# Hybrid encoder trunk: the mixers' input renewed ahead of the values, and half of the mixing weights' second parts made by a copy and an adding transfer

## The chip, the cores and the metric

One core of a Trainium2 chip. The metric is device time in microseconds (us) of one execution; a kernel's time is the median of three runs, and beside them stands one profiled execution, from which every row of the trace is taken.

## The reference

Two layers over an input of 512 tokens and 1024 channels. In each, three token mixers read the same normed input, their outputs are merged by gates, and a feed-forward block and an embedding gate follow.

```python
h = rmsnorm(x, mix_norm[i])
z = h @ w_in[i]
u_rnn, u_gelu, c_q, ckv_rope, fq, fk, fv, f_logit, gate_logit = split_columns(z)
y_a = rglru_branch(u_rnn, u_gelu, ...) @ w_br_a[i]     # causal conv of width 4, gates, recurrence
y_b = mla_branch(c_q, ckv_rope, ...) @ w_br_b[i]       # latent attention, 8 heads
y_c = fox_branch(fq, fk, fv, f_logit, fox_bf[i]) @ w_br_c[i]  # 8 heads, forget-gate bias
g = sigmoid(gate_logit + gate_b[i]).reshape(B, S, 3, D)
merged = g[:, :, 0] * y_a + g[:, :, 1] * y_b + g[:, :, 2] * y_c
x = x + merged @ w_o[i]
...                                                     # SwiGLU block, then x += sigmoid(.) * (p[i] @ w_ple[i])
```

The recurrence is `h = a h + b` with `a = exp(log_a)` and `b = sqrt(1 - a^2) * (gate * conv)`. All is float32.

## The kernel before, in words

**Precision.** A float32 operand is held as two float32r parts, first (`h`, hi) and second (`l`, lo = value minus first). Each product of a 128x128 weight tile with 128x512 of activations is three matmuls (`mm3`): hi by hi, hi by lo, lo by hi.

**Weights.** All weights come as one stream of 606 units, each of four tiles (128x512, 256 KB). SP's queue loads a unit into `raw` (4 slots). `Stream._split` makes the parts in `hl` (8 slots): ScalarE casts the first (line 112), VectorE subtracts for the second (line 113). `_ensure` splits unit u+7 when unit u is begun.

**Pages.** Activations lie in SBUF pages: `pf` (20 of 128x512 float32) and `pr` (31 of two float32r parts). Eight PSUM banks of 128x512.

**One layer's mixing** (`mix`). The input of the mixers is eight pages X, made at first without the norm's factor: x times the gain, split. The factor per token, r (a page `st["r"]`, as a column `rT`), is known only later, so that what is computed from X is multiplied by r when it leaves PSUM ("rescaled"). In program order: four tile columns for the convolution branch (u), the packed columns of rotary key and forget logits, four for the gelu branch (ug), the recurrence's gates, `lru_tail` (square roots, products and scans of the recurrence, with the last of VectorE's scans at line 677), key and query of the first head pair (`fox_proj`), the values of the fox attention (`values`: eight units of 12 matmuls, into four banks at once), then `attention`. `lru_tail` stands ahead of the first heads in the kernel before already.

**Attention** runs over head and query block; each step does the scores, the softmax (VectorE, ScalarE) and, with TensorE free meanwhile, some tiles of independent work taken from a plan: `fp(p, w)` is key or query of head pair p, `mg(n, j)` a merge gate with its branch column, `lq` and `lkv` latent projections.

**Renewal.** `renorm(ks)` loads x again from DRAM through POOL's queue, multiplies it by gain and r (line 218, a scalar_tensor_tensor on VectorE) and splits it (line 233 on ScalarE, line 221 on VectorE) into new pages Xn. Nothing computed from Xn needs rescaling. In the kernel before it stands in three pieces in the first plan of the fox attention, between fills that still use X and r; `drop_x` then frees X and r.

**Order.** Each engine works through its instructions in order. A framework's scheduler sets that order per engine from the program and its dependences; `high_priority` around the weight splits lets them go ahead. Where below the order of an engine is printed, a row is line, operation, output and inputs, and what it waits for (an engine's count, with the suffix of its semaphore); `DMASW` is a transfer issued by POOL, `DMAHW` one issued by SP. `bank_67` to `bank_74` are the PSUM banks.

Of the kernel before, what the change touches and what calls it, by code (L numbers as in the profile page):

```python
# [10 lines left out]
F32 = mybir.dt.float32  # L11
F32R = mybir.dt.float32r
I32 = mybir.dt.int32
AF = mybir.ActivationFunctionType
ALU = mybir.AluOpType
# [3 lines left out]
KD = D // 128  # L19
# [18 lines left out]

NUNITS = 606
KEPT = NUNITS - 16  # L40
PACKED = (8, 9, 311, 312)


# [41 lines left out]
class Stream:  # L85
# [15 lines left out]
    def _split(self, u):  # L101
        s = (u % self.nraw) * 512
        src = self.raw[:, s:s + 512]
        if u >= KEPT:
            self.kept[u] = self.pages.take()
        hi, lo = self._parts(u)
        if u in PACKED:
            hi, lo = (x.rearrange("p (k c) -> p k c", c=128)[:, :, 64 * i:64 * i + 64]
                      for i, x in ((0, hi), (1, hi)))
            src = src.rearrange("p (k c) -> p k c", c=128)[:, :, 0:64]  # L110
        with self.tc.high_priority():
            self.nc.scalar.copy(hi, src)  # L112
            self.nc.vector.tensor_tensor(lo, src, hi.bitcast(F32), op=ALU.subtract)  # L113

    def _parts(self, u, c=slice(0, 512)):
        if u in self.kept:
# [5 lines left out]
    def _ensure(self, u):  # L122
        last = min(u + self.nhl - 1, max(u + 4, KEPT - 1), NUNITS - 1)
        while self.loaded < min(self.nraw, NUNITS):
            self._load(self.loaded)
            self.loaded += 1
        while self.done <= last:
            self._split(self.done)
            self.done += 1
            while self.loaded < min(self.done + self.nraw, NUNITS):  # L130
                self._load(self.loaded)
                self.loaded += 1
# [34 lines left out]
class Trunk:  # L167
# [273 lines left out]
    def mix(self, layer):  # L441
        nc = self.nc
        L, st, X = layer, self.st, self.xp
# [42 lines left out]
        rT = self.cols(NT)  # L486
# [24 lines left out]
        def key_and_forget():  # L511
# [3 lines left out]
            for k, x in enumerate(X):  # L515
                assert self.w.pos // 4 in PACKED
                wh, _ = self.w.tile(("kf", L, k))
# [84 lines left out]
        def fox_proj(p, X, r):  # L602
            return [
                self.dense(self.win(L, C_FK + 128 * p), X, ev_heads(kp, p, r, True, False)),
                self.dense(self.win(L, C_FQ + 128 * p), X, ev_heads(qp, p, r, True, True)),
            ]

        def values(spec, X, rT):

            V = []  # L610
            bs = [self.banks.take() for _ in range(NT)]
            for k, x in enumerate(X):
                wh, wl = self.w.wide(spec + (k,))
                for j in range(NT):
                    c = slice(j * 128, (j + 1) * 128)
                    self.mm3(bs[j][:, :], x.h[:, c], x.l[:, c], wh, wl, k == 0, k == len(X) - 1)
                    yield
            for j in range(NT):
                g = pr.take()
                V.append(g)  # L620
                dst = g.ap.rearrange("p (h t d) -> p h t d", h=HEADS, t=2)
                src = bs[j].rearrange("p (h d) -> p h d", h=HEADS)
                hi = dst[:, :, 0, :]
                if rT is None:
                    self.split(hi, dst[:, :, 1, :], src)
                else:
                    r = rT[:, j:j + 1]
                    self.act(hi, src, AF.Copy, scale=r)
                    self.stt(dst[:, :, 1, :], src, r, hi.bitcast(F32), ALU.mult, ALU.subtract)
                self.banks.give(bs[j])  # L630
            self.V = V


        yA = [None] * 4
# [50 lines left out]
        k0, q0 = fox_proj(0, X, st["r"])  # L685
        self.run(k0)
        self.run(q0)
        self.run(values(("fv", L), X, rT))
        Xn = [None] * KD

        def renorm(*ks):

            for k in ks:
                t, p = pf.take(), pr.take()
                nc.gpsimd.dma_start(t.ap, x_dram[k])
                self.stt(t.ap, t.ap, self.v(L, V_MIX + k), st["r"].ap, ALU.mult, ALU.mult)
                self.split(p.h, p.l, t.ap)
                t.free()
                Xn[k] = p
            return  # L700
            yield

        def drop_x():
            for p in X:
                p.free()
            st.pop("r").free()
            return
            yield


        merged = [None] * KD
        out_pages = [None] * KD
# [32 lines left out]
        def merge(n, j, ys, X=Xn, r=None):  # L745
            box = []
            yield from gate(n, j, box, X, r)
            yield from branch(n, j, ys, box)
# [154 lines left out]
        def fp(p, w, X=Xn, r=None):  # L903
            return (fox_proj(p, X, r)[w], 8)

        def mg(n, j, ys, X=Xn, r=None):
            return (merge(n, j, ys, X, r), 12)
# [56 lines left out]
        def done_c():  # L964
            for p in oC:
# [5 lines left out]
        lkv = [(latent(ckv, skv, C_CKV, j), 8) for j in range(2)]  # L971
        tail = chain(gate(2, 2, boxes[2, 2]), gate(2, 3, boxes[2, 3]))
        attention(True, oC, [
            [fp(1, 0, X, st["r"]), (renorm(0, 1), 0), mg(0, 0, yA, X, st["r"]), (renorm(2, 3, 4), 0),
             mg(0, 1, yA, X, st["r"]), (renorm(5, 6, 7), 0), (drop_x(), 0), fp(1, 1), mg(0, 2, yA)],
            [fp(2, 0), mg(0, 3, yA), mg(0, 4, yA), fp(2, 1), mg(0, 5, yA)],
            [fp(3, 0), mg(0, 6, yA), fp(3, 1)] + lq,
            lkv + [mg(0, 7, yA), (free_yA(), 0), (latent_sums(), 0), gt(2, 0), (latent_norm(), 0),
# [160 lines left out]
    def ple_last(self, X, pw):  # L1139

        L, st = DEPTH - 1, self.st
        self.w.align()
        assert self.w.pos == 4 * KEPT
        fin = [{}, {}]
        half = [slice(0, SEQ // 2), slice(SEQ // 2, SEQ)]

        def part(i, j):
            t = half[i]
            b = self.banks.take()
            for k in range(KD):  # L1150
                if i == 0:
                    wh, wl = self.w.tile(("w_ple_gate", L, 128 * j, 128, k))
                else:
                    wh, wl = self.w.again(4 * KEPT + KD * j + k)
                self.mm3(b[:, :SEQ // 2], wh, wl, X[k].h[:, t], X[k].l[:, t], k == 0, k == KD - 1)
# [236 lines left out]
```

## Time and profile before

| | |
|---|---|
| median of three runs | 1826.25 us (1825.64 to 1828.06) |
| the profiled execution | 1826.21 us; span 1824.4 us, granted clock 0.994 |
| matmul records | 8476 |
| stream of weights (SP's queue) | 606 loads of 256 KB |
| second parts by subtraction (line 113) | 590 records, 404.4 us of VectorE |
| first parts by cast (line 112) | 590 records, 363.8 us of ScalarE |

A page row of busy time gives for each engine us, share of the span and number of instructions. Timeline rows give start, length, engine, line, operation, output and inputs, how many, and in brackets the idle time ahead with what ended it. PE is TensorE's matmul, PEld its weight load, DVE VectorE, ACT ScalarE, POOL GpSimd. Granted clock is the share of TensorE's full clock.

### The profile page before, as it was taken

Reading aid. Unit: us, or ns where it says so; the run is one execution under the profiler, and the core shown is the slowest. Engines: PE = TensorE matmul, PEld = TensorE weight load, DVE = VectorE, ACT = ScalarE, POOL = GpSimd, SP = SyncE. Lnnn points to the kernel's source line nnn. Section 1 sums busy time; section 2 is a strip of 40 time slices with the busy share of each in tenths; the row PEclk is TensorE's granted clock in tenths of the full one; section 3 lists DMA queues with packets and bytes.
Section 4 is the critical chain, followed back from the end, with each engine's and each line's share of the span. In section 5 each row is a group of like instructions: output and inputs, shape, how many; then the busy total and the mean of one; then the engine's idle time right before and its main releaser. Section 6 shows DMA issues by size and latency. Waiting matters only on the chain. (4 is left out here: it accounts for less than half of the span.)

```text
span 1824.4 us, 24163 instructions
## 1 busy us (share of the span) xinstructions
PE 1803.9 (99%) x8476; PEld 1504.5 (82%) x8476; DVE 1209.1 (66%) x2421; ACT 817.5 (45%) x1562; POOL 116.8 (6%) x234
## 2 busy tenths in 40 slices
PE   9899999999999999999999999999999999999998
PEld 7688888888888888888888788888888888888887
DVE  8896678866665555444778966888576555553457
ACT  5766556553333333223448655565523333332233
POOL 1230001100000000000103200010000000000000
PEclk9899999999999999999999999999999999999999
DMA  6142224324322233322433322342232323232331
GB/s 206 59 150 83 81 78 116 100 70 139 95 96 95 96 99 98 109 95 98 133 111 123 105 81 82 90 117 85 87 128 92 99 98 97 95 110 99 98 99 47
DMA packets 98826, 184.17 MB, mean 101 GB/s; under 512 B 13552, under 2 KB 14752, under 8 KB 98704
## 3 DMA queue, kind: packets, MB, share of 16 engines
q1 hardware_dynamic: 89280, 162.04, 27.3%
q0 software_dynamic: 8416, 19.45, 3.9%
q8 instruction: 66, 1.08, 0.2%
q10 hardware_dynamic: 1008, 1.14, 0.2%
q14 instruction: 56, 0.46, 0.1%
HBM read 173.98 MB, written 4.21 MB: 98 GB/s over the span
## 5 line engine op out<-in xcount | busy, mean ns | idle before, releaser
L237 PE MATMUL bank<-pr,hl 128*128 128x512 f32 (+1 forms) x6812 | 1602.3, 392 | 7.0 <-ACT pr L233 6.9
L237 PEld LDWEIGHTS bank<-pr,hl 128*128 128x128 f32 (+1 forms) x6812 | 1270.0, 188 | 268.9 <-ACT pr L233 8.6
L112 ACT CAST hl<-raw 128x512 fp32r<-128x512 f32 x590 | 363.8, 618 | 649.4 <-PE bank L237 438.8
L113 DVE TENSOR_TENSOR hl<-raw,hl 128x512 fp32r<-128x512 f32 x590 | 404.4, 686 | 367.9 <-ACT hl L112 352.0
L221 DVE TENSOR_TENSOR pf<-pf 128x512 f32<-128x512 f32 (+3 forms) x235 | 151.2, 651 | 31.9 <-ACT pf L230 29.8
L221 DVE TENSOR_TENSOR pf<-bank,pf 128x512 f32<-128x512 f32 (+3 forms) x198 | 132.9, 676 | 56.9 <-PE bank L237 31.9
L230 ACT ACTIVATE pf<-pf 128x512 f32<-128x512 f32 (+1 forms) x145 | 86.0, 600 | 112.3 <-DVE pf L221 110.0
L237 PE MATMUL bank<-pr 128*128 128x256 f32 (+5 forms) x704 | 119.5, 301 | 3.5 <-ACT pf L230 3.3
L237 PEld LDWEIGHTS bank<-pr 128*128 128x128 f32 (+1 forms) x704 | 103.4, 190 | 13.7 <-ACT pf L230 3.4
L221 DVE TENSOR_TENSOR pr<-pf,pr 128x512 fp32r<-128x512 f32 (+3 forms) x126 | 85.5, 683 | 4.0 <-ACT pr L233 3.1
L230 ACT ACTIVATE pf<-bank,small 128x384 f32<-128x384 f32 (+3 forms) x130 | 68.9, 531 | 42.0 <-DVE small L838 38.6
L233 ACT CAST pr<-pf 128x512 fp32r<-128x512 f32 (+2 forms) x114 | 70.3, 620 | 29.2 <-DVE pf L218 18.1
L855 ACT CAST pth<-bank 128x128 fp32r<-128x128 f32 (+3 forms) x128 | 54.0, 426 | 65.4 <-PE bank L830 62.3
L838 DVE TENSOR_REDUCE small<-bank 128x1 f32<-128x384 f32 (+3 forms) x128 | 61.7, 484 | 19.2 <-PE bank L237 18.2
L221 DVE TENSOR_TENSOR ptl<-bank,pth 128x128 fp32r<-128x128 f32 (+3 forms) x128 | 61.7, 484 | 12.8 <-ACT pth L855 10.3
L237 PE MATMUL bank<-hl,pr 128*128 128x512 f32 x240 | 55.9, 390 | 0.0
L830 PE MATMUL bank<-identr,pf 128*128 128x128 f32 x320 | 55.7, 273 | 0.0
L237 PEld LDWEIGHTS bank<-hl,pr 128*128 128x128 f32 x240 | 44.9, 188 | 9.2
L225 DVE TENSOR_SCALAR pf<-pf,small 128x384 f32<-128x384 f32 (+3 forms) x128 | 48.4, 383 | 2.6
L230 ACT ACTIVATE pf<-bank,vec 128x512 f32<-128x512 f32 x60 | 41.0, 688 | 16.7 <-PE bank L237 16.2
L218 DVE SCALAR_TENSOR_TENSOR pf<-pf,bank 128x512 f32<-128x512 f32 x48 | 32.6, 683 | 20.8 <-PE bank L237 20.5
L830 PEld LDWEIGHTS bank<-identr,pf 128*128 128x128 f32 x320 | 40.0, 141 | 7.6
(112 smaller groups left out, 792.9 us busy)
## 6 DMA issues: line engine op xcount, KB each, us to landing
raw<-wst SPq DMA_DIRECT2D x606, 256.0 KB, 2.6
pf<-xT POOLq DMA_DIRECT2D x16, 256.0 KB, 3.1
pr<-pr POOLq DMA_DIRECT2D x32, 128.0 KB, 2.7
pf<-xs POOLq DMA_DIRECT2D x16, 256.0 KB, 3.1
pf<-trig POOLq DMA_DIRECT2D x12, 256.0 KB, 3.1
pf<-xT SPq DMA_DIRECT2D x8, 256.0 KB, 5.4
xs<-pf POOLq DMA_DIRECT2D x8, 256.0 KB, 2.7
pf<-pT POOLq DMA_DIRECT2D x4, 256.0 KB, 3.1
```

The source lines that it names most:

```text
L112: self.nc.scalar.copy(hi, src)
L113: self.nc.vector.tensor_tensor(lo, src, hi.bitcast(F32), op=ALU.subtract)
L218: self.nc.vector.scalar_tensor_tensor(out, a, s, b, op0=op0, op1=op1)
L221: self.nc.vector.tensor_tensor(out, a, b, op=op)
L225: self.nc.vector.tensor_scalar(out, a, s1, None, op0=op0)
L230: return self.nc.scalar.activation(out, a, f, **kw)
L233: self.nc.scalar.copy(hi, src)
L237: self.nc.tensor.matmul(out, a, b, start=start, stop=stop, skip_group_check=True)
L830: nc.tensor.transpose(T[:, c], p2.ap[:, c], self.ident[:, :])
L838: nc.vector.reduce_max(R[t][:, 0:1], S[:, :m], axis=AX.X, negate=True)
L855: self.nc.scalar.copy(hi, src)
```

## The change

Two edits. First, units in `ADDED` (every odd unit from 11 to 129 and from 315 to 433, 120 of 606, those of the two layers' mixing) get their second part in another way: ScalarE writes minus the first part into the second's place, and a transfer issued by POOL adds the unit's weights from DRAM to it. VectorE's subtraction is left out for these; the cast and the load into `raw` stay. Second, the renewal of all eight pages stands ahead of the values, X and r are dropped behind them, and the fills of the first plan that used X and r (one projection and two merges per layer) read Xn and lose their rescaling.

```diff
--- before.py
+++ after.py
@@ -38,6 +38,8 @@
 
 NUNITS = 606
 KEPT = NUNITS - 16
+
+ADDED = {*range(11, 130, 2), *range(315, 434, 2)}
 PACKED = (8, 9, 311, 312)
 
 
@@ -110,7 +112,13 @@
             src = src.rearrange("p (k c) -> p k c", c=128)[:, :, 0:64]
         with self.tc.high_priority():
             self.nc.scalar.copy(hi, src)
-            self.nc.vector.tensor_tensor(lo, src, hi.bitcast(F32), op=ALU.subtract)
+            if u in ADDED:
+
+                self.nc.scalar.activation(lo, hi.bitcast(F32), AF.Copy, scale=-1.0)
+                c = 512 * (u % 2)
+                self.nc.gpsimd.dma_start(lo, self.wdram[u // 2][:, c:c + 512], accum_op=ALU.add)
+            else:
+                self.nc.vector.tensor_tensor(lo, src, hi.bitcast(F32), op=ALU.subtract)
 
     def _parts(self, u, c=slice(0, 512)):
         if u in self.kept:
@@ -685,7 +693,6 @@
         k0, q0 = fox_proj(0, X, st["r"])
         self.run(k0)
         self.run(q0)
-        self.run(values(("fv", L), X, rT))
         Xn = [None] * KD
 
         def renorm(*ks):
@@ -697,16 +704,15 @@
                 self.split(p.h, p.l, t.ap)
                 t.free()
                 Xn[k] = p
-            return
-            yield
 
         def drop_x():
             for p in X:
                 p.free()
             st.pop("r").free()
-            return
-            yield
-
+
+        renorm(*range(KD))
+        self.run(values(("fv", L), X, rT))
+        drop_x()
 
         merged = [None] * KD
         out_pages = [None] * KD
@@ -971,8 +977,7 @@
         lkv = [(latent(ckv, skv, C_CKV, j), 8) for j in range(2)]
         tail = chain(gate(2, 2, boxes[2, 2]), gate(2, 3, boxes[2, 3]))
         attention(True, oC, [
-            [fp(1, 0, X, st["r"]), (renorm(0, 1), 0), mg(0, 0, yA, X, st["r"]), (renorm(2, 3, 4), 0),
-             mg(0, 1, yA, X, st["r"]), (renorm(5, 6, 7), 0), (drop_x(), 0), fp(1, 1), mg(0, 2, yA)],
+            [fp(1, 0), mg(0, 0, yA), mg(0, 1, yA), fp(1, 1), mg(0, 2, yA)],
             [fp(2, 0), mg(0, 3, yA), mg(0, 4, yA), fp(2, 1), mg(0, 5, yA)],
             [fp(3, 0), mg(0, 6, yA), fp(3, 1)] + lq,
             lkv + [mg(0, 7, yA), (free_yA(), 0), (latent_sums(), 0), gt(2, 0), (latent_norm(), 0),
```

The lines move by 8 behind the first edit: 113 becomes 121, 218 becomes 226, 221 becomes 229, 233 becomes 241, 237 becomes 245, 677 becomes 685, 695 becomes 702.

What moves on the engines, at three places in layer 0. TensorE, from the last block of the values on; `bank<-hl,pr` rows are values, `bank<-pr` rows are attention scores, and `bank<-pr,hl` rows are fills. Before:

```order
L237 MATMUL bank_72<-hl,pr 128x512 x3
L237 MATMUL bank_73<-pr 128x128 [waits Activation_49]
L237 MATMUL bank_73<-pr 128x128 [waits DMASW0_49,DMASW2_49,DVE_49,Pool_49]
L237 MATMUL bank_68<-pr,hl 128x512 x21
L237 MATMUL bank_69<-pr 128x256 x2
L237 MATMUL bank_68<-pr,hl 128x512 x3
L237 MATMUL bank_70<-pr,hl 128x512 x14
L237 MATMUL bank_70<-pr,hl 128x512 [waits DVE_49]
L237 MATMUL bank_70<-pr,hl 128x512 x3
L237 MATMUL bank_71<-pr 128x384 [waits DVE_49]
```

and now:

```order
L245 MATMUL bank_72<-hl,pr 128x512 x3
L245 MATMUL bank_73<-pr 128x128 [waits DVE_49,Activation_49]
L245 MATMUL bank_68<-pr,hl 128x512
L245 MATMUL bank_68<-pr,hl 128x512 [waits DVE_49]
L245 MATMUL bank_68<-pr,hl 128x512
L245 MATMUL bank_69<-pr 128x256
L245 MATMUL bank_70<-pr,hl 128x512 [waits DVE_49]
L245 MATMUL bank_70<-pr,hl 128x512
L245 MATMUL bank_70<-pr,hl 128x512 [waits DVE_49]
L245 MATMUL bank_73<-pr 128x128 [waits DMASW1_49,DMASW3_49,DVE_49,Pool_49]
L245 MATMUL bank_69<-pr 128x256
L245 MATMUL bank_71<-pr 128x384 [waits DVE_49]
```

Before, the first fill (bank_68) goes through all its blocks of X without a wait, 24 matmuls, and the second follows it; now the first blocks of two fills (banks 68 and 70) are followed by work that waits for VectorE. Further on, the second parts of the first fill's second block (the last row) stand behind more waits for VectorE, and wait for it themselves:

```order
L245 MATMUL bank_72<-pr,hl 128x512 [waits DVE_49]
L245 MATMUL bank_72<-pr,hl 128x512
L245 MATMUL bank_72<-pr,hl 128x512 [waits DMASW5_49]
L245 MATMUL bank_67<-pr,hl 128x512 [waits DVE_49]
L245 MATMUL bank_67<-pr,hl 128x512
L245 MATMUL bank_68<-pr,hl 128x512 [waits Activation_49]
L245 MATMUL bank_70<-pr,hl 128x512
L245 MATMUL bank_72<-pr,hl 128x512
L245 MATMUL bank_73<-pr 128x512 [waits Activation_49]
L245 MATMUL bank_73<-pr 128x512
L245 MATMUL bank_68<-pr,hl 128x512 [waits DVE_49]
```

VectorE, where the values leave their banks (`pr<-bank,small,pr` rows). `pf<-pf,vec` rows are the multiplication of a renewed page, `pr<-pf,pr` rows the second half of a split, and `hl<-raw,hl` rows the weight subtraction. Before:

```order
L218 SCALAR_TENSOR_TENSOR pf<-pf,vec 128x512 [waits DMASW1_49]
L113 TENSOR_TENSOR hl<-raw,hl 128x512 [waits DMAHW7_49,Activation_49]
L218 SCALAR_TENSOR_TENSOR pf<-pf,vec 128x512 [waits DMASW2_49]
L218 SCALAR_TENSOR_TENSOR pr<-bank_71,small,pr 128x8x64 [waits Activation_49]
L221 TENSOR_TENSOR pr<-pf,pr 128x512 [waits Activation_49]
L218 SCALAR_TENSOR_TENSOR pr<-bank_74,small,pr 128x8x64 [waits Activation_49]
L221 TENSOR_TENSOR bank_73<-bank_73,fmask 128x128 [waits PE_49]
L218 SCALAR_TENSOR_TENSOR pf<-pf,vec 128x512 [waits DMASW3_49]
L218 SCALAR_TENSOR_TENSOR pr<-bank_67,small,pr 128x8x64 [waits Activation_49]
L221 TENSOR_TENSOR pr<-pf,pr 128x512 [waits Activation_49]
L113 TENSOR_TENSOR hl<-raw,hl 128x512 [waits DMAHW0_49,Activation_49]
```

and now:

```order
L226 SCALAR_TENSOR_TENSOR pr<-bank_74,small,pr 128x8x64 [waits Activation_49]
L226 SCALAR_TENSOR_TENSOR pr<-bank_67,small,pr 128x8x64 [waits Activation_49]
L226 SCALAR_TENSOR_TENSOR pr<-bank_72,small,pr 128x8x64 [waits PE_49,Activation_49]
L229 TENSOR_TENSOR bank_73<-bank_73,fmask 128x128 [waits PE_49]
L229 TENSOR_TENSOR bank_69<-bank_69,fmask 128x128 [waits PE_49]
L226 SCALAR_TENSOR_TENSOR pf<-pf,vec 128x512 [waits DMASW3_49]
L229 TENSOR_TENSOR pr<-pf,pr 128x512 [waits Activation_49]
L229 TENSOR_TENSOR bank_71<-bank_71,fmask 128x128 [waits DVE_49,PE_49]
L226 SCALAR_TENSOR_TENSOR pf<-pf,vec 128x512 [waits DMASW4_49]
L844 TENSOR_REDUCE small<-bank_73 128x1 [waits DVE_49]
L844 TENSOR_REDUCE small<-bank_69 128x1 [waits DVE_49]
L229 TENSOR_TENSOR pr<-pf,pr 128x512 [waits Activation_49]
```

Ahead of the first row shown stands the evacuation of the first bank. Of the renewal's eight multiplications six stand ahead of it now and two behind it, five and three before; the last row is the split of page 1, the second of the eight. From the first `SCALAR_TENSOR_TENSOR` of the recurrence behind the scan of the forget gates (line 537, now 545) to this row stand 55 instructions, both counted: 4 scans, 8 multiplications of renewed pages, 4 evacuations of values, 3 masks, 2 reductions, 5 weight subtractions and 29 others of 512 columns.

POOL, around the forget gates' logarithm (lines 376 to 379, now 384 to 387). Before:

```order
L378 TENSOR_SCALAR pf<-pf 128x32 [waits Pool_49]
L379 TENSOR_TENSOR pf<-pf 128x32 [waits Pool_49]
L534 DMA pf<-pf 8x16x32 [waits DVE_49,Activation_49]
L589 DMA pr<-pr 2x1x512 [waits DMASW0_49,DVE_49]
L589 DMA pr<-pr 2x1x512 [waits DMASW1_49]
```

and now:

```order
L386 TENSOR_SCALAR pf<-pf 128x32 [waits Pool_49]
L387 TENSOR_TENSOR pf<-pf 128x32 [waits Pool_49]
L542 DMA pf<-pf 8x16x32 [waits DMASW7_49,DVE_49]
L119 DMA hl<-wst 128x512 [waits DMASW0_49,PE_49,Activation_49]
L702 DMA pf<-xT 128x512 [waits DMASW7_49,DMASW1_49]
L595 MEMSET pr 4x512 [waits PE_49,Pool_49]
L119 DMA hl<-wst 128x512 [waits DMASW2_49,Activation_49]
L702 DMA pf<-xT 128x512 [waits DMASW3_49,DVE_49]
L702 DMA pf<-xT 128x512 [waits DMASW4_49]
```

The eight loads of x (line 695) stood in one run behind six small transfers of the head pages (line 589), two of which are shown. Now they (line 702) follow the logarithm's transfer at once, with adding transfers (line 119) and memsets of the head pages between them; the first add shown is that of unit 27, which waited its turn behind the whole logarithm.

## The prediction

> **What bounds the kernel now.** I read the engine shares first, then TensorE's waits, then windows and timelines around the places that these point to.
>
> The page, busy time and slices:
>
> ```profile
> PE 1803.9 (99%) x8476; PEld 1504.5 (82%) x8476; DVE 1209.1 (66%) x2421; ACT 817.5 (45%) x1562; POOL 116.8 (6%) x234
> ...
> PEclk9899999999999999999999999999999999999999
> ```
>
> The waits of TensorE (us in total, times, longest):
>
> ```profile
> PE bank L237 <- ACT pr L233: 6.9, 3, 3.8
> PE bank L237 <- ACT pf L230: 3.3, 1, 3.3
> PE bank L237 <- DVE one L385: 1.0, 1, 1.0
> PE bank L237 <- ACT raw L230: 0.9, 1, 0.9
> ```
>
> TensorE is the bound. The first two rows are all that matters inside the program; the third belongs to its start, the fourth to its end. A change that touches no matmul can win only there, so its value must be read from two places. The windows of 8 us at them (columns: PE, PEld, DVE, ACT, POOL, granted clock, DMA share, GB/s), with one undisturbed window first:
>
> ```profile
> 44.00:52.00 8.00, 8.00 (x37) 6.63 (x36) 8.00 (x16) 4.54 (x8) 0.63 (x1) 1.00 0.15 44
> 52.00:60.00 8.00, 3.65 (x15) 2.36 (x13) 8.00 (x15) 3.78 (x7) 0.00 (x0) 0.98 0.24 71
> 60.00:68.00 8.00, 5.47 (x12) 3.87 (x13) 8.00 (x15) 4.89 (x8) 0.00 (x0) 0.50 0.18 61
> 68.00:76.00 8.00, 8.00 (x32) 6.48 (x32) 5.18 (x11) 8.00 (x15) 4.90 (x13) 0.88 0.13 35
> ...
> 1018.00:1026.00 8.00, 4.83 (x14) 3.85 (x15) 7.91 (x16) 5.13 (x11) 3.29 (x7) 0.79 0.34 107
> ```
>
> 37 matmuls go into 8 us, 0.216 us each. Layer 0 lost 111-59 = 52 of them from 52 to 76, 11.2 us: 6.9 of waiting and 4.3 of clock at 0.50. Layer 1 lost 23, 5.0 us: 3.3 of waiting, 1.7 of clock. So the prize is 16.2 us at most. VectorE is full (8.00 of 8) in both. TensorE's timeline:
>
> ```profile
> 49.77 5.15 PE L237 MATMUL bank<-pr,hl 128*128 128x512 f32 x22
> 58.72 0.73 PE L237 MATMUL bank<-pr,hl 128*128 128x512 f32 x2 [3.81 <-ACT pr L233]
> 60.69 1.22 PE L237 MATMUL bank<-pr,hl 128*128 128x512 f32 x2 [1.23 <-ACT pr L233]
> 63.75 18.61 PE L237 MATMUL bank<-pr,hl 128*128 128x512 f32 x68 [1.84 <-ACT pr L233]
> 82.21 21.92 PE L237 MATMUL bank<-hl,pr 128*128 128x512 f32 x96
> 103.97 0.33 PE L237 MATMUL bank<-pr 128*128 128x128 f32 x2
> ...
> 975.84 21.92 PE L237 MATMUL bank<-hl,pr 128*128 128x512 f32 x96
> 997.60 0.22 PE L237 MATMUL bank<-pr 128*128 128x128 f32 x1
> ...
> 1021.17 0.73 PE L237 MATMUL bank<-pr 128*128 128x512 f32 x2 [3.29 <-ACT pf L230]
> ```
>
> The x96 blocks are the values. Behind them TensorE finds attention work ready at once, since its first fills read the old X pages. VectorE at the same time (the POOL rows are the logarithm that precedes the scan of the forget gates):
>
> ```profile
> 70.08 0.31 POOL L376 TENSOR_SCALAR pf<-pf 128x32 f32<-128x32 f32 x1 [23.90 <-DVE pf L221]
> 77.67 0.25 POOL L379 TENSOR_TENSOR pf<-pf 128x32 f32<-128x32 f32 x1
> 79.03 0.71 POOL L534 DMA_DIRECT2D pf<-pf  x1 [1.10 <-DVE pf L218]
> ...
> 81.14 1.22 DVE L537 TENSOR_TENSOR_SCAN pf<-one,pf 8x512 f32<-8x512 f32 x1 [0.78 <-DMA pf<-pf]
> 82.39 0.69 DVE L113 TENSOR_TENSOR hl<-raw,hl 128x512 fp32r<-128x512 f32 x1
> 85.31 1.31 DVE L218 SCALAR_TENSOR_TENSOR pf<-pf 128x512 f32<-128x512 f32 x2 [0.79 <-ACT pf L230]
> 92.10 1.22 DVE L677 TENSOR_TENSOR_SCAN pf<-pf 128x512 f32<-128x512 f32 x1
> 93.24 0.66 DVE L113 TENSOR_TENSOR hl<-raw,hl 128x512 fp32r<-128x512 f32 x1
> 93.82 0.68 DVE L218 SCALAR_TENSOR_TENSOR pf<-bank,pf 128x512 f32<-128x512 f32 x1
> 94.42 0.68 DVE L113 TENSOR_TENSOR hl<-raw,hl 128x512 fp32r<-128x512 f32 x1
> ...
> 111.75 0.28 DVE L221 TENSOR_TENSOR bank<-bank,fmask 128x128 f32<-128x128 f32 x1
> 111.95 0.73 DVE L218 SCALAR_TENSOR_TENSOR pf<-pf,vec 128x512 f32<-128x512 f32 x1
> 112.61 0.74 DVE L218 SCALAR_TENSOR_TENSOR pr<-bank,small,pr 128x512 fp32r<-128x512 f32 x1
> ...
> 982.38 1.29 DVE L218 SCALAR_TENSOR_TENSOR pf<-pf 128x512 f32<-128x512 f32 x2
> ```
>
> The 85.31 row begins the recurrence (the products behind the square roots); call its start T. In layer 1 T is 982.38. From start to start, a scan takes 1.14 us, a plain 128x512 operation 0.60, one with a per-partition column (`vec`, `small`) 0.66, a mask 0.20.
>
> **The adding transfers.** 120 subtractions leave VectorE, 120 negated copies join ScalarE, 120 transfers join POOL's queue. Prices:
>
> ```profile
> L113 DVE TENSOR_TENSOR hl<-raw,hl 128x512 fp32r<-128x512 f32 x590 | 404.4, 686 | 367.9 <-ACT hl L112 352.0
> L230 ACT ACTIVATE pf<-pf 128x512 f32<-128x512 f32 (+1 forms) x145 | 86.0, 600 | 112.3 <-DVE pf L221 110.0
> ...
> pf<-xT POOLq DMA_DIRECT2D x16, 256.0 KB, 3.1
> ...
> pf<-xT SPq DMA_DIRECT2D x8, 256.0 KB, 5.4
> ```
>
> VectorE loses 120 x 0.686 = 82 us, ScalarE gains 120 x 0.600 = 72, POOL at most 120 x 0.71 = 85 of issuing (the 79.03 row). All of it lies beside TensorE except where the two stalls are: cost 0. No row shows an adding transfer. The nearest are 3.1 us (256 KB on POOL) and 5.4 (256 KB on SP at the start); I take 3.1, the same queue. The cover is the lead: a unit is split 7 units ahead of its 12 matmuls, 7 x 12 x 0.216 = 18 us. Behind a busy POOL the add can come late. The tightest is unit 27, queued behind the logarithm (some 8 us), with a landing at about 82, while TensorE wants its second part in the fourth value block, 80.4 + 3 x 2.74 = 88.6. That leaves 6 us; at 5.4 us a landing 4 are left. Gone, it would be a wait of TensorE for each microsecond over, in every unit of that stretch.
>
> A page of the Trainium skill speaks against such transfers: SBUF — State Buffer, "SBUF: two separate sides", says that a transfer issued from GpSimd needs descriptors written through a port that VectorE's two-port operations lock, and gives about 3.1 us in place of 0.62 for one that overlaps such an operation. By it an add here might land some 2.5 us later (estimate), and the sum would not move, but the chance of rival (c) would be some 0.2. The x pages land in 3.1 us although VectorE is full while they come, so the trace does not bear the rule out, and (c) keeps 0.10.
>
> **The convolution's end, layer 0.** TensorE waits at 54.9 to 63.75 for splits behind a full VectorE. In the new order two subtractions fewer (2 x 0.60) stand ahead of them, and the first result reaches VectorE three matmuls earlier (3 x 0.216): 1.8 us, between 0 and 3. The values then end at 103.97 - 1.8 = 102.2.
>
> **The renewal, layer 0.** The new first fills read the renewed pages. The first fill may use page 0 early, but its second block wants page 1, whose split is the last but one of the renewal on VectorE, behind the four evacuations of the values. From T to that split VectorE has 55 instructions: 4 scans, 12 of 0.66, 5 masks and reductions of about 0.22, 34 of 0.60 (5 of them weight subtractions): 4.6 + 7.9 + 1.1 + 20.4 = 34.0. T itself is not set by VectorE's load but by the logarithm, its transfer and the scan: 1.8 us earlier, two memsets inside POOL's chain (0.3 each, its other rows' size), and no subtraction between scan and T: 70.08-1.8+7.84+0.6 = 76.7, transfer issued at 77.9, landed 2.1 later as before (79.03 to 81.14), scan 1.2: T = 81.4 (80 to 84; the late end if ScalarE, 8.00 of 8 from 68 to 76, with its negated copies holds the square roots back). Page 1 is ready at 115.4. TensorE without a wait would stand there 32 matmuls behind the values, six of them narrow: 102.2 + 6.3 = 108.5. New wait: 6.9, in pieces of which the longest is some 4.
>
> **The renewal, layer 1.** Values end at 997.60 as before, since TensorE did not wait ahead of them. VectorE's share from T to page 1's split is 60 instructions, 13 short ones: 4 x 1.14 + 12 x 0.66 + 31 x 0.60 + 13 x 0.25 = 34.3. T is bounded by ScalarE and the scan; fewer subtractions let the logarithm start sooner, ScalarE's square roots hardly: 980.4 (979 to 982.4). Ready at 1014.7; TensorE would be there at 997.6 + 35 matmuls, 7.0, = 1004.6. New wait 10.1. The old loss of 5.0 goes: the heads' VectorE work then no longer competes with the renewal.
>
> **Clock.** Idle time lowers the clock: 4.3 us lost in layer 0 beside 6.9 of waiting, 1.7 in layer 1 beside 3.3. For the new waits I take 2.0 and 2.5, nearest to the second since most of the slow stretch falls into the waiting; bounds 0 and 4.3 each.
>
> The Trainium skill, TensorE: Matmul & The Clock Gate, "What's actually happening", has the half clock after an idle window of about 3.4 us and until a busy one of 3.4. By that each place would lose about 1.7 us (estimate), and the sum would come out 1.1 us lower. The trace agrees in layer 1 (1.7) but not in layer 0 (4.3), where short bursts lay between waits.
>
> **The rescaled evacuations.** Three groups per layer lose an operation of 0.60 on VectorE, inside the count above. POOL loads the eight x pages in both; they land before their turn.
>
> **Sum.** Layer 0: -1.8 + 6.9 + 2.0 = +7.1. Layer 1: -5.0 + 10.1 + 2.5 = +7.6. The profiled execution took 1826.2 us (span 1824.4 and 1.8 around it), equal to the median of 1826.25. 1826.2 + 14.7 = 1840.9, say 1841. Its own range, with all low ends and all high ends: -3.0+5.5-5.0+8.7 = +6 and 9.5+4.3-5.0+12.1+4.3 = +25: 1832 to 1851.
>
> **Rivals.** (a) Faster: the relief of VectorE pulls T forward so far that all pages are renewed under the values. It decides if T is at 74.5 and 970.3 or sooner with the same 34 us. Then the two stalls shrink by 1.8 and 5.0 and nothing new comes: 1819.4. For it: 82 us off VectorE where it is full. Against it: VectorE is already idle 0.78 and 0.79 ahead of scan and T, waiting for a transfer and ScalarE.
> (b) No change: the new waits come out near 3.4 us each with little clock, since TensorE's first fills find some pages early; gains and waits cancel at 1826. That needs T 4 to 6 us sooner than I have it.
> (c) Much slower: the adding transfers land late, behind POOL's in-order waits or because an add is dearer than a copy. The point is 6 us more at unit 27, or over 5.2 us each if they go one after another (a unit pair lasts 24 x 0.216). One microsecond over that in all 120 is +120; only behind the logarithm, two units per layer, about +10: 1851, and I call 1860 its time. Only the 5.4 row speaks for it.
> (d) The adds come to nothing, VectorE being no faster at the places that count: that is my own forecast but for the 1.8; 1843, inside its range.
>
> **Chances.** Forecast with (d) 0.69, (a) 0.13, (b) 0.08, (c) 0.10. A measurement tells 0.2%, 3.7 us, from no change. Faster 0.13, same 0.08, slower 0.79. The range 1825 to 1855 holds forecast, (b) and the mild part of (c); outside are (a) and the dear part of (c).
>
> **What would show it.** Right: a TensorE wait for L229 or L241 pieces of 4 us and more behind each values block, at about 104 and 1000; VectorE at 8.00 of 8 from T to 115; the 1021 wait gone; adds landing in about 3 us and no wait for a transfer. Wrong: no wait behind the values (T early), or waits for `hl` from a transfer.

## The result and the profile after

The changed kernel takes 1842.59 us (median of 4 runs, 1840.59 to 1843.63) where the kernel before takes 1827.13 on the same count (1825.64 to 1828.06): a ratio of 1.0084, 95% interval 1.0067 to 1.0102. It is slower by 15.5 us. The profiled execution took 1840.59 us, its span is 1838.8, 14.4 more than before.

The page of the changed kernel, busy time and the adding transfers (KB each, median us from issue to landing):

```profile
PE 1809.2 (98%) x8476; PEld 1506.4 (82%) x8476; DVE 1140.6 (62%) x2295; ACT 881.0 (48%) x1682; POOL 219.5 (12%) x354
...
hl<-wst POOLq DMA_DIRECT2D x120, 256.0 KB, 4.2
```

VectorE lost 68.5 us of work (1209.1 to 1140.6), and the kernel is slower all the same. TensorE's waits (us in total, times, longest) say where:

```profile
PE bank L245 <- DVE pr L226: 12.6, 4, 6.9
PE bank L245 <- ACT pr L241: 5.7, 5, 2.3
...
PE bank L245 <- DVE pr L229: 0.8, 1, 0.8
```

The first and the last row are new. There line 226 on VectorE is the evacuation of the values out of their banks, and line 229 the split of a renewed page. The waits at the convolution's end (line 241 in layer 0) are smaller, and the 3.3 us wait of layer 1 for the softmax is gone. The windows (PE, PEld, DVE, ACT, POOL, clock, DMA share, GB/s):

```profile
52.00:60.00 8.00, 4.57 (x17) 2.92 (x16) 8.00 (x15) 4.74 (x9) 0.85 (x1) 0.94 0.66 149
60.00:68.00 8.00, 7.36 (x21) 5.04 (x21) 7.55 (x17) 6.59 (x11) 0.41 (x2) 0.63 0.04 15
...
100.00:108.00 8.00, 2.76 (x13) 1.87 (x12) 7.94 (x13) 7.09 (x14) 4.31 (x10) 0.93 0.97 237
108.00:116.00 8.00, 5.44 (x12) 3.97 (x13) 8.00 (x17) 2.49 (x4) 1.83 (x4) 0.50 0.43 110
...
1006.00:1014.00 8.00, 2.66 (x10) 1.61 (x9) 8.00 (x15) 6.23 (x12) 3.14 (x6) 0.84 1.08 308
1014.00:1022.00 8.00, 6.37 (x19) 4.54 (x17) 8.00 (x19) 5.41 (x12) 1.48 (x3) 0.74 0.15 41
```

From 52 to 68 there are 38 matmuls in place of 27. From 100 to 116 there are 25, where 37 go into each 8 us undisturbed. VectorE is full or nearly so in all of them (7.55 of 8 at the least). TensorE's timeline, both layers:

```profile
61.42 17.50 PE L245 MATMUL bank<-pr,hl 128*128 128x512 f32 x66 [0.64 <-ACT pr L241]
78.76 21.92 PE L245 MATMUL bank<-hl,pr 128*128 128x512 f32 x96
...
102.85 0.47 PE L245 MATMUL bank<-pr 68*128 68x128 f32 x2 [0.56 <-issue]
110.25 1.01 PE L245 MATMUL bank<-pr 128*128 128x384 f32 x2 [6.94 <-DVE pr L226]
111.57 6.96 PE L245 MATMUL bank<-pr,hl 128*128 128x512 f32 x18 [0.31 <-DVE pr L226]
...
118.83 5.38 PE L245 MATMUL bank<-pr,hl 128*128 128x512 f32 x23
...
983.23 21.92 PE L245 MATMUL bank<-hl,pr 128*128 128x512 f32 x96
1010.66 0.62 PE L245 MATMUL bank<-pr 128*128 128x384 f32 x2 [3.88 <-DVE pr L226]
...
1012.97 5.44 PE L245 MATMUL bank<-pr,hl 128*128 128x512 f32 x12 [1.46 <-DVE pr L226]
...
1021.19 0.98 PE L245 MATMUL bank<-pr,hl 128*128 128x512 f32 x3 [1.63 <-ACT pr L241]
...
1023.78 10.49 PE L245 MATMUL bank<-pr,hl 128*128 128x512 f32 x45 [0.76 <-DVE pr L229]
```

The values start 3.45 us earlier in layer 0 (82.21 to 78.76) and 7.39 later in layer 1 (975.84 to 983.23), so layer 0 cost 7.4 us net; the other 7.0 of the 14.4 come in layer 1. VectorE at the start of the recurrence, at the evacuation of the values and at the split of page 1:

```profile
79.53 1.22 DVE L545 TENSOR_TENSOR_SCAN pf<-one,pf 8x512 f32<-8x512 f32 x1 [2.01 <-DMA pf<-pf]
80.78 1.29 DVE L226 SCALAR_TENSOR_TENSOR pf<-pf 128x512 f32<-128x512 f32 x2
...
109.45 2.72 DVE L226 SCALAR_TENSOR_TENSOR pr<-bank,small,pr 128x512 fp32r<-128x512 f32 x4
...
115.14 0.69 DVE L229 TENSOR_TENSOR pr<-pf,pr 128x512 fp32r<-128x512 f32 x1
...
984.55 1.22 DVE L545 TENSOR_TENSOR_SCAN pf<-one,pf 8x512 f32<-8x512 f32 x1 [2.84 <-DMA pf<-pf]
...
988.49 0.75 DVE L226 SCALAR_TENSOR_TENSOR pf<-pf,vec 128x512 f32<-128x512 f32 x1 [1.29 <-DMA pf<-xs]
989.16 1.29 DVE L226 SCALAR_TENSOR_TENSOR pf<-pf 128x512 f32<-128x512 f32 x2
...
1023.03 1.30 DVE L229 TENSOR_TENSOR pr<-pf,pr 128x512 fp32r<-128x512 f32 x2
```

From the first product of the recurrence to the end of page 1's split VectorE works 35.0 us in layer 0 (80.78 to 115.8) and 34.5 in layer 1 (989.16 to 1023.7) without a pause. TensorE has stood still or gone slowly since 103 and 1007.

### The profile page after: what moved, and what is told of

Same layout as the page of the kernel before. It is cut to its first block, busy times and chain, and to the rows that moved or that the text cites. A ratio compares the mean times of both kernels' runs of the same rounds, so it can differ in the third digit from the quotient of the medians.

```text
span 1838.8 us, 24284 instructions
## 1 busy us (share of the span) xinstructions
PE 1809.2 (98%) x8476; PEld 1506.4 (82%) x8476; DVE 1140.6 (62%) x2295; ACT 881.0 (48%) x1682; POOL 219.5 (12%) x354
## 4 chain that ended last, share of the span: by engine, by line
PE 93%; DVE 4%; POOL 1%; DMA 1%; issue 1%; ACT 0%; DVEq 0%; POOLq 0%
PE bank L245 91%; PE bank L836 2%; DVE pf L226 1%; DVE pr L229 1%; DVE pf L685 0%; DVE pf L229 0%; DMA pf<-pf 0%; DVE hl L121 0%; POOL pf L386 0%; POOL pf L387 0%; DVE pr L226 0%; DMA pf<-xs 0%; ACT pr L574 0%; ACT hl L114 0%; DVE small L844 0%
## 5 line engine op out<-in xcount | busy, mean ns | idle before, releaser
L121 DVE TENSOR_TENSOR hl<-raw,hl 128x512 fp32r<-128x512 f32 (+1 forms) x470 | 322.8, 687 | 358.1 <-ACT hl L114 342.6
L229 DVE TENSOR_TENSOR pf<-pf 128x512 f32<-128x512 f32 (+3 forms) x235 | 151.7, 653 | 31.7 <-ACT pf L238 29.5
L229 DVE TENSOR_TENSOR pf<-bank,pf 128x512 f32<-128x512 f32 (+3 forms) x192 | 128.9, 677 | 63.6 <-PE bank L245 31.6
L119 POOL DMA_DIRECT2D hl<-wst x120 | 107.0, 892 | 478.8 <-ACT hl L117 380.7
L245 PE MATMUL bank<-pr 128*128 128x256 f32 (+4 forms) x704 | 120.6, 302 | 11.4 <-DVE pr L226 10.8
L229 DVE TENSOR_TENSOR pr<-pf,pr 128x512 fp32r<-128x512 f32 (+2 forms) x122 | 82.6, 684 | 6.9 <-ACT pr L241 6.3
L238 ACT ACTIVATE pf<-bank,small 128x512 f32<-128x512 f32 (+3 forms) x130 | 69.0, 532 | 32.8 <-DVE small L844 29.0
L241 ACT CAST pr<-pf 128x512 fp32r<-128x512 f32 (+1 forms) x114 | 70.0, 618 | 28.8 <-DVE pf L226 17.8
L229 DVE TENSOR_TENSOR ptl<-bank,pth 128x128 fp32r<-128x128 f32 (+3 forms) x128 | 61.9, 487 | 25.2 <-ACT pth L861 20.9
L844 DVE TENSOR_REDUCE small<-bank 128x1 f32<-128x128 f32 (+3 forms) x128 | 62.2, 488 | 24.4 <-PE bank L245 23.1
L117 ACT ACTIVATE hl<-hl 128x512 fp32r<-128x512 f32 x120 | 75.9, 632 | 2.0
L229 DVE TENSOR_TENSOR bank<-bank,fmask 128x128 f32<-128x128 f32 x64 | 19.0, 298 | 54.5 <-PE bank L245 54.0
```

What stands on the lines that cost most here:

```text
L117: self.nc.scalar.activation(lo, hi.bitcast(F32), AF.Copy, scale=-1.0)
L119: self.nc.gpsimd.dma_start(lo, self.wdram[u // 2][:, c:c + 512], accum_op=ALU.add)
L229: self.nc.vector.tensor_tensor(out, a, b, op=op)
L238: return self.nc.scalar.activation(out, a, f, **kw)
L245: self.nc.tensor.matmul(out, a, b, start=start, stop=stop, skip_group_check=True)
L844: nc.vector.reduce_max(R[t][:, 0:1], S[:, :m], axis=AX.X, negate=True)
```

## Experiments

Theory A: the adding transfers cost nothing and win a few us at both old stalls; the loss is the renewal, because the first fills now read pages that VectorE finishes late. Its rivals are that the adds make the loss (B), that VectorE is late for the values' evacuation whatever TensorE reads (C), and that POOL's queue delivers late once more is asked of it (D). The adds alone, the renewal alone, the early renewal with fills on X, and the adds in two places are set against 16 runs of the kernel before (1826.14 us median), the other four against 12 runs (1826.34).

### The adds alone

```diff
# the kernel before, with
+ADDED = {*range(11, 130, 2), *range(315, 434, 2)}
 ...
+            if u in ADDED:
+                self.nc.scalar.activation(lo, hi.bitcast(F32), AF.Copy, scale=-1.0)
+                c = 512 * (u % 2)
+                self.nc.gpsimd.dma_start(lo, self.wdram[u // 2][:, c:c + 512], accum_op=ALU.add)
+            else:
                 # the subtraction on VectorE, as before
```

> The adding transfers alone; the renewal and the first plan stand as in the kernel before. Theory A (the loss comes from the renewed pages, the adds cost nothing): the values of layer 0 start at 78.8 as in the changed kernel (82.2 before), no wait for VectorE behind the values, the wait at 1021 smaller or gone: 1827 - 3.4 - (0 to 5) = 1819 to 1824. Rival B (the adds themselves cost TensorE, by late landings or a busy ScalarE): 1827 or more, with waits for a transfer or for ScalarE's cast that the kernel before does not have.

Measured: 1818.92 us, ratio 0.9959 (0.9947 to 0.9972). TensorE's waits inside the program are one row, and the values stand at

```profile
PE bank L245 <- ACT pr L241: 2.9, 2, 2.3
```

```profile
80.42 21.92 PE L245 MATMUL bank<-hl,pr 128*128 128x512 f32 x96
...
973.40 21.92 PE L245 MATMUL bank<-hl,pr 128*128 128x512 f32 x96
```

The values start 1.8 us earlier in layer 0, as the prediction had it (the expectation had 3.4, from the changed kernel's own trace, and the time is at the low end of its range). The wait at 1021 is gone and no other takes its place. Theory A holds for this half: the adds are worth 7 us. B falls.

### The renewal alone

```diff
# the changed kernel, with
-ADDED = {*range(11, 130, 2), *range(315, 434, 2)}
+ADDED = set()
```

> The renewal ahead of the values alone; all second parts are subtracted on VectorE as before. Theory A: the recurrence starts at 85.3 as before, and VectorE has 4 subtractions more (2.4 us) in front of page 1: ready at 85.3 + 34.2 + 2.4 = 121.9 where TensorE would stand at 110.3, so 11.6 of waiting and 2 to 4 of clock in layer 0; in layer 1 982.4 + 36.7 = 1019 against 1004.6, 14.5 and 2 to 4, less the old 5.0: 1827 + 25 to 29 = 1852 to 1856. Rival B (the adds make the loss): about 1827.

Measured: 1847.88 us, ratio 1.0118 (1.0104 to 1.0132), 22 us slower. The waits and the values:

```profile
PE bank L245 <- DVE pr L226: 10.7, 4, 5.7
PE bank L245 <- ACT pr L241: 8.2, 4, 3.8
PE bank L245 <- POOL pr L595: 4.2, 1, 4.2
```

```profile
80.91 21.92 PE L245 MATMUL bank<-hl,pr 128*128 128x512 f32 x96
...
120.95 5.28 PE L245 MATMUL bank<-pr,hl 128*128 128x512 f32 x22 [0.64 <-DVE pr L229]
...
985.43 21.92 PE L245 MATMUL bank<-hl,pr 128*128 128x512 f32 x96
```

The sign and the place are those of theory A, the size is 4 us below the expected range. The miss lies in layer 0, which costs 9.6 net (975.84 to 985.43) where 13.6 to 15.6 was expected; layer 1 costs the other 12.2, inside its 11.5 to 13.5. In layer 0 the reader of page 1 goes on at 120.95, 12.0 us after the 109.0 (80.91 + 21.76 + 6.3) at which TensorE could have been there, and its last wait is for page 1's split. So the lateness is about the expected 11.6, the slow clock lies inside it, and I had added 2 to 4 for the clock on top. Ahead of the values 1.3 us were won (last section), and 1.1 come back behind, by what is open. The third row, a wait for POOL to clear a head page in layer 1, is not what sets the loss: a wait for a split (L229) ends behind it, at 1029.6. The two halves nearly add up: -7.2 for the adds and +21.7 for the renewal make 14.5, against 15.5 for both.

### The renewal early, but the first fills read X

```diff
# the changed kernel, with (drop_x is a step of the plan again)
-        drop_x()
 ...
-            [fp(1, 0), mg(0, 0, yA), mg(0, 1, yA), fp(1, 1), mg(0, 2, yA)],
+            [fp(1, 0, X, st["r"]), mg(0, 0, yA, X, st["r"]), mg(0, 1, yA, X, st["r"]), (drop_x(), 0), fp(1, 1), mg(0, 2, yA)],
```

> The changed kernel with adds and with all eight pages renewed ahead of the values, but the first projection and the first two merges read X and are rescaled by r as before, and X is dropped behind them. VectorE's order up to the evacuation of the values is that of the changed kernel. Theory A (TensorE waits since its first fills read renewed pages and since only three short fills stand ahead of the score that needs the first bank of the values): the 7 us waits behind both values go, the gain of 3.4 at the convolution's end stays, the old wait at 1021 may come back: 1819 to 1824. Rival C (the renewal ahead of the values keeps VectorE so long that the evacuation of the values itself is late, whatever TensorE reads): TensorE still waits 5 us and more for the first bank in each layer, 1830 to 1840.

Measured: 1820.73 us, ratio 0.9969 (0.9957 to 0.9982). The waits, and VectorE's evacuation of the first banks in layer 0:

```profile
PE bank L245 <- ACT pr L241: 4.4, 4, 2.3
PE bank L245 <- ACT pf L238: 1.1, 1, 1.1
```

```profile
110.35 2.06 DVE L226 SCALAR_TENSOR_TENSOR pr<-bank,small,pr 128x512 fp32r<-128x512 f32 x3
```

VectorE still evacuates the values late (110.35 in layer 0, 109.45 in the changed kernel), and no wait for it is left: the score that waited 6.94 us for the first bank now stands behind 46 matmuls, nearly all of them fills on X, in place of 10. So an early renewal does next to no harm by itself (1820.73 against 1818.92 with the adds alone), C falls, and what costs is that the first fills need its result. This one edit takes back 22 us.

### One fill in three reads X

```diff
# the changed kernel, with (drop_x is a step of the plan again)
-        drop_x()
 ...
-            [fp(1, 0), mg(0, 0, yA), mg(0, 1, yA), fp(1, 1), mg(0, 2, yA)],
+            [fp(1, 0, X, st["r"]), (drop_x(), 0), mg(0, 0, yA), mg(0, 1, yA), fp(1, 1), mg(0, 2, yA)],
```

> The changed kernel, but the first projection of the first plan (24 matmuls, 5.2 us) reads X and is rescaled; the two merges behind it read the renewed pages. Theory A (the loss is the time by which VectorE's renewal ends later than TensorE runs out of other work, so each fill that does not need it takes its own length off): some 21 matmuls or 4.5 us more lie ahead of the first renewed block in each layer, so the loss falls by 4.5 and a part of the clock's per layer: 1842.5 - 9 to 13 = 1829 to 1833. Rival C (any fill that reads renewed pages stops TensorE as long as before): 1838 to 1843.

Measured: 1832.43 us, ratio 1.0032 (1.0020 to 1.0045), inside the range of theory A.

```profile
PE bank L245 <- DVE pr L226: 5.9, 5, 2.5
...
PE bank L245 <- DVE pr L229: 2.2, 2, 1.8
```

10 of the 22 us come back with 24 matmuls per layer, 5.2 us of work in each. By the two profiled executions, which lie 8.3 us apart, it is 5.9 in layer 0 (layer 1's values start at 977.32 in place of 983.23) and 2.4 in layer 1. So the loss goes down by about the length of the work that does not need the renewed pages, over both layers together; layer by layer it does not come out so evenly.

### More adds at the front, in two places

```diff
# the adds alone, with
-ADDED = {*range(11, 130, 2), *range(315, 434, 2)}
+ADDED = {*range(10, 34), *range(313, 337)}
```

> The kernel before with adding transfers for all units from 10 to 33 and 313 to 336 (24 in each layer, odd and even), none later. Theory A: four subtractions fewer still ahead of the convolution's end, so layer 0's stall shrinks by up to 2.4 us more than with every other unit; the renewal in the attention is as crowded as before, so the wait at 1021 stays: 1818 to 1824. Rival D (POOL's queue, with an add each 2.6 us and the forget gates' logarithm of 8 us in it, delivers late): waits for a transfer of some us at the values, 1827 to 1835.

Measured: 1822.02 us, ratio 0.9979 (0.9970 to 0.9987). The wait for a transfer, and the values of layer 0:

```profile
PE bank L245 <- DMA hl<-wst: 2.3, 1, 2.3
```

```profile
77.18 21.92 PE L245 MATMUL bank<-hl,pr 128*128 128x512 f32 x96
```

POOL ahead of that wait, in layer 1:

```profile
984.57 0.56 POOL L703 DMA_DIRECT2D pf<-xs  x1 [1.15 <-DVE pf L685]
985.13 0.94 POOL L119 DMA_DIRECT2D hl<-wst  x1
```

Both mechanisms show: the values start 3.2 us sooner than with every other unit, and in layer 1 they wait 2.3 us for an add (at 992), where four adds are issued from 985 to 990, among and behind loads of x that waited for VectorE. The expectation had the wait at 1021 stay, since no unit is added in the attention (the last add is issued at 990). It is gone here too; in the attention only waits of 0.8 us and less for VectorE are left.

### Adds for all of the first units in layer 0, every other one elsewhere

```diff
# the adds alone, with
-ADDED = {*range(11, 130, 2), *range(315, 434, 2)}
+ADDED = {*range(10, 23), *range(23, 130, 2), *range(315, 434, 2)}
```

> The adds alone, and in layer 0 every unit from 10 to 22 is added, not every other one; none of these adds comes due behind the forget gates' logarithm. Theory A (layer 0's stall shrinks with each subtraction taken from ahead of the convolution's end): the values start at 77.2 as with adds for all of 10 to 33, 80.4 with every other; no late add: 1818.9 - 3.2 = 1815 to 1817. Rival D (the added ScalarE and POOL work there gives the gain back): 1818.5 to 1820.

Measured: 1816.63 us, ratio 0.9947 (0.9934 to 0.9959), the fastest of all, 9.7 us under the kernel before and 26 under the changed one.

```profile
PE bank L245 <- ACT pr L241: 3.6, 3, 1.9
```

```profile
77.26 21.92 PE L245 MATMUL bank<-hl,pr 128*128 128x512 f32 x96
```

The start of the values is the expected one, with no wait for a transfer. Its interval and that of the adds alone overlap, so the 2.3 us between the two are likely, not shown.

### Adds for every unit

```diff
# the adds alone, with
-ADDED = {*range(11, 130, 2), *range(315, 434, 2)}
+ADDED = {*range(10, 130), *range(313, 434)}
```

> The adds alone, for every unit from 10 to 129 and from 313 to 433, 241 in place of 120. Theory A (transfers hide as long as POOL delivers): layer 0's stall as small as in the run with 24 units per layer, values at 77.2, and in both layers a wait for late adds behind the logarithm of about 2 us: 1817 to 1822. Rival D (an adding transfer each 2.6 us is more than the queue or its engines carry at a landing of 4 to 5 us): waits for transfers in many units, 1830 to 1900.

Measured: 1821.81 us, ratio 0.9974 (0.9963 to 0.9985).

```profile
PE bank L245 <- DMA hl<-wst: 4.6, 2, 3.5
...
hl<-wst POOLq DMA_DIRECT2D x241, 256.0 KB, 4.7
```

241 adds still hide, but for one wait in each layer: 1.1 us in layer 0, in the fills behind the values, and 3.5 us in layer 1, among the values. POOL also loads x at both places. So the queue carries far more than 120 adds; only lateness at a busy place costs, and D is true only there.

### The price of adding

```diff
# the adds alone, with
-                self.nc.gpsimd.dma_start(lo, self.wdram[u // 2][:, c:c + 512], accum_op=ALU.add)
+                self.nc.gpsimd.dma_start(lo, self.wdram[u // 2][:, c:c + 512])
```

> The adds alone, but each adding transfer is a plain copy of the same 256 KB into the same place by the same queue, so the second parts are the weights themselves (the product is another one; the work and the order are the same). Theory A (adding costs the transfer engines a second pass over the data): the landing falls from 4.2 us to 3.1 to 3.4 and the queue's share of the 16 engines from 14.9% to 3.9 + 31.5 MB at the weights' 0.17% each = 9%. Rival B (the queue is only busier, adding costs nothing): landing 4.2 and share 14 to 15% as with the adds. Time in both: 1819, within 1.

One execution took 1819.22 us. The adds (first) and the plain copies (second), the landing, the queue and the issue on POOL:

```profile
hl<-wst POOLq DMA_DIRECT2D x120, 256.0 KB, 4.2
...
q0 software_dynamic: 25696, 50.91, 14.9%
...
L119 POOL DMA_DIRECT2D hl<-wst x120 | 107.5, 896 | 475.0 <-ACT hl L117 383.0 <-ACT pth L863 41.4 <-ACT pf L238 15.5
```

```profile
hl<-wst POOLq DMA_DIRECT2D x120, 256.0 KB, 3.2
...
q0 software_dynamic: 25696, 50.91, 10.2%
...
L119 POOL DMA_DIRECT2D hl<-wst x120 | 65.0, 542 | 500.5 <-ACT hl L117 417.1 <-ACT pth L863 40.4 <-PE bank L245 13.4
```

Adding costs 1.0 us of landing, 4.7 points of the 16 DMA engines' time for the same bytes, and 0.35 us more of POOL per issue; none of it reaches TensorE, whose waits inside the program are 2.9 us with both. The Trainium skill, DMA: Bandwidth & Descriptors, "Rules for kernel authors", says that an accumulating transfer reads its destination and writes it later; the dearer landing agrees with that, though no run here looks inside a transfer. The plain copies land in 3.2 us beside the same full VectorE, so the 2.5 us that the prediction weighed for a locked descriptor port do not show here either. No run tells whether what VectorE did here locks that port at all, so the rule itself is not tested.

## Why the prediction was right

The forecast, 1841, lies 1.6 us under the measurement. The place, the sign and the main mechanism are those that the runs bear out: VectorE's queue behind the recurrence is too long for what TensorE reads first. That the sum comes so close is partly luck, since errors of 1 to 2.3 us in its terms cancel. Its steps:

- **The adding transfers cost nothing.** Right (the adds alone: no wait for a transfer). Their price was not: 4.2 us of landing where I took 3.1, and 107 us of issuing on POOL where I had 85 as a bound. The lead covered both. VectorE lost 68.5 us where I had 82, ScalarE gained 63.5 where I had 72; nothing hung on it.
- **The convolution's end, -1.8.** The adds alone show 1.8, the changed kernel's profile 3.45. The match of the first is luck: TensorE's waits there shrink by 4.0 us with the adds alone (6.9 to 2.9), and slow matmuls take the rest back. In the changed kernel the waits end 2.3 us earlier (61.42 for 63.75), and the rest of the 3.45 is clock, 0.63 for 0.50 from 60 to 68 (last section).
- **T.** 80.78 for 81.4 in layer 0 (the steps that I gave add up to 81.2); in layer 1 981.8 (989.16 less the 7.39 of layer 0) for 980.4, since the forget gates' scan and the first renewed page, ahead of it on VectorE, waited for their transfers (the 984.55 and 988.49 rows). Inside the bounds.
- **55 and 60 instructions, 34 us.** 35.0 and 34.5.
- **Page 1 late by 6.9 and 10.1.** Its lateness, the time from where TensorE could have stood without a wait to the end of page 1's split, was under-estimated. In layer 0 it is 115.8 less 106.8 (78.76 + 21.76 + 6.3): 9.0, mostly since TensorE came 1.7 sooner. In layer 1 the fill goes on at 1023.78, and TensorE would have stood there at 1004.99 + 7.0 = 1012.0: 11.8, and its last wait, 0.76, is for this split.
- **Page 1 sets the loss.** Right in layer 1, wrong in layer 0. In layer 0 its reader is the row at 118.83 (32 matmuls behind the values, as forecast), 3.0 us after the split had ended, with no idle time ahead of it. Of the 12.0 us by which TensorE came late to it, 7.8 are waits: 0.56, then 6.94 for the first bank of the values and 0.31 for another bank. The other 4.2 are slow matmuls, with the clock at 0.50 from 108 to 116. The evacuations stand a few us ahead of page 1's split in the same queue of VectorE, so the cause is the queue that the prediction counted, but the instruction that TensorE waited for is another.
- **The clock, 2.0 and 2.5.** In layer 0 the slow clock carried TensorE 3.0 us past the end of the split: -3.45 + 9.0 + 3.0 = 8.6, of which 1.2 come back ahead of layer 1's values, by what is open; net 7.39. Layer 1 cost 7.0: -5.0 + 11.8 leaves 0.2, since the slow clock there fell into the time that page 1 was late. So 2.0 stood for 3.0, and 2.5 for next to nothing.
- **The old 5.0 in layer 1 goes.** Right, and it took less than the reason that I gave: the wait at 1021 goes with the adds alone, where the renewal still competes with the heads, with the renewal alone (0.8 us is left of waits for ScalarE's line 238), and with 24 adds at the front of each layer.
- **Where TensorE stands.** I looked for waits for L229 or L241 of 4 us and more at about 104 and 1000. They begin at 103 and 1007 and are 6.94 and 3.88 us long, but both are for L226, the first bank of the values.

The rival of a faster kernel asked for T at 74.5 in layer 0; it came at 80.78. That rival's gain does exist, in the kernel with adds and the old plan.

## What to carry to other kernels

A busy share that falls by 68 us says nothing as long as the engine is full where another waits for it: find the last instruction that the waiting engine needs, and count the queue in front of it. When a preparation is moved ahead, look at who reads its result first; keeping the first readers (one projection and two merges per layer) on the old operand cost one multiplication per evacuation here and was worth 22 us. Where a wait and a slow clock stand together, compare the time at which the operand is ready with the time at which the engine gets there: a slow clock inside the lateness costs nothing more (layer 1), but it can carry the engine past it (3.0 us in layer 0).

## What the runs showed of the hardware beyond this

The same waits at the convolution's end cost different amounts. In the renewal alone they are 3.81, 1.23 and 1.84 us, as in the kernel before, yet the values start 1.3 us sooner; the clock stood at 0.57 in place of 0.50, and at 1.00 in place of 0.88 in the next window:

```profile
60.00:68.00 8.00, 5.25 (x14) 3.73 (x15) 8.00 (x15) 4.67 (x8) 0.00 (x0) 0.57 0.19 64
68.00:76.00 8.00, 8.00 (x37) 6.64 (x36) 5.33 (x11) 8.00 (x15) 5.25 (x13) 1.00 0.10 34
```

Added up over the three windows from 52 to 76, the clock lost 8 x (0.02 + 0.50 + 0.12) = 5.1 us of full speed in the kernel before and 8 x 0.43 = 3.4 here. The other profiles show the same few sizes: 5.1 with the adds alone (0.88, 0.50, 0.98), 3.4 in the changed kernel (0.94, 0.63, 1.00), 1.7 with adds for every unit (1.00, 0.79, 1.00), and none lies between. So the slow clock came in steps of about 1.7 us. One step is also what separates the 3.45 us of the changed kernel from the 1.8 of the adds alone at this place. The Trainium skill, TensorE: Matmul & The Clock Gate, "What's actually happening", says that the window which decides on the clock runs freely, so that the moment of a change depends on where in it the first matmul lands. The steps fit that, with the end of a wait in place of the kernel's start; one profile of each kernel can't tell it from another cause. A difference of 1 to 2 us between two kernels that have such a stall can come from this alone.
